# Windowed attention in a fused two-block kernel: four heads of one key head a step, values split into one stationary tile, score matmuls ordered by issue edges

## The chip, the core and the metric

The kernel runs on one core of one Trainium2 chip. The engines that matter here are TensorE (PE: matmuls and transposes, with its own sequencer for weight loads, PEld), VectorE (DVE), ScalarE (ACT) and SyncE (SP, which issues the DMAs). The metric is the device time of one launch in microseconds; three runs of the kernel before took 3067.52, 3069.00 and 3069.83 us, median 3069.0.

## The reference

512 tokens of 1024 channels pass two hybrid layers and then a second block (gated MLP mixing, a gated linear recurrence, a feed-forward part), all in float32. In each hybrid layer a convolution branch, a retention branch and a windowed attention branch read the same normalised input, are gated, added and projected. The change touches the attention branch alone:

```python
def window_attention_branch(q, k, v, gate, q_norm_g, k_norm_g, sink, positions):
    G = ATTN_HEADS // ATTN_KV_HEADS          # 16 // 4
    T = ATTN_BLOCK                           # 128
    q = rotary(rms_norm(q.reshape(B, S, ATTN_HEADS, HEAD_DIM), q_norm_g), ...)
    k = rotary(rms_norm(k.reshape(B, S, ATTN_KV_HEADS, HEAD_DIM), k_norm_g), ...)
...
    s = jnp.einsum('bhgnqj,...', qb, kwin) * (HEAD_DIM ** -0.5)   # 128 queries x 3 blocks of keys
    s = jnp.where(valid, s, -1e30)           # |kpos - qpos| <= 128
    m = jnp.maximum(jnp.max(s, axis=-1, keepdims=True), sink_l)
    p = jnp.exp(s - m)
    p = p / (jnp.sum(p, axis=-1, keepdims=True) + jnp.exp(sink_l - m))
    o = jnp.einsum('bhgnqj,bnjhd->bnqhgd', p, vwin)
    return o.reshape(B, S, ATTN_HEADS * HEAD_DIM) * jax.nn.silu(gate)
```

Sixteen query heads of 64 share four key and value heads, four to one. A block of 128 queries sees its own block of keys and the two beside it: 256 keys for the first and the last block, 384 for the two between.

## The kernel before

**Arithmetic.** Every float32 operand of a matmul is held as two parts, hi and lo, whose product sum `mm3` (L172 to L174) forms with three matmuls: hi by hi, hi by lo, lo by hi. A "dense" matmul below is one of these, a 128x128 stationary tile by 512 columns. `split` makes the two parts from PSUM: a cast on ACT (L205) and a subtraction on DVE (L206). Weights arrive by DMA in chunks of 128x1024 and are split in the same way by ACT (L149) and DVE (L150).

**Attention.** A layer calls `att_core(l, g)` twice (g = 0, 1), here "first core" (A) and "second core" (B). A core has eight steps, one for each of four query blocks n and two groups pp of four heads, and is a pipeline of three stages. In iteration `it` of its loop stand, in the order of the code: the value matmuls V of step it-2 with the gate product (four `stt` of 64x128, L213), the transposes T (L771) and splits of step it-1, and the score matmuls S (L792) of step it with its softmax. S of a step is 12 matmuls of 256 or 384 columns that contract 64 rows, into four PSUM tiles, one a head, two query tiles of two heads each; heads of both key heads of a call stand in one step, since the key tile holds one key head on its upper 64 partitions and the other on its lower 64. Softmax: a fused mask-add and row maximum on DVE (L794), the maximum against the sink (nm, L213, and es, L210, 128x4), four exps on ACT with row sums (L223), the exp of the sink, sum and reciprocal (L210, L808), and the scaling of four probability tiles, two on DVE (L217), two on ACT (L223). T turns a block of 128 keys of four heads, four 128x128 transposes into one PSUM tile, and a split of 128x512 follows. V multiplies for each block of keys the transposed probabilities (512 columns, four heads) by the values of two key heads, three matmuls by `mm3`; the upper half of the product is valid for two heads and the lower half for the other two, which is why the gate product goes in halves. After the loop four `ya` tiles are split and later read by the branch's output projection ("ao").

**What sets the order.** Every `yield` hands control to a weaver, which places 24 dense matmuls of the convolution branch between two iterations. A scheduler then orders each engine's instructions by readiness and priority from the order of the code, so that the final order on an engine need not be that of the code; each engine then works its list strictly in order. From the second core on the 31 taps of the depthwise convolution (`stt` of 128x4xx to 512 from SBUF, L213) are fed to DVE in small portions. PSUM has three pools: mm (2 buffers, names pm), acc (4, pa: scores among others) and misc (2, pi: transposes and values). `tc.issue_after(x)` puts the instructions made inside it behind x.

`att_kv` and `att_kT` make keys and values: four PSUM tiles of tokens give values in `av` (two pairs of hi and lo tiles) and, through norm and rotation, keys that `att_T` (L673) transposes into two key tiles a layer.

The lines that the change replaces in the loop are these:

```python
vh, vl = av[jb // 2]
self.mm3(ps, vh[:, c:c + 128], vl[:, c:c + 128], ph, pl, x == 0, x == len(pt) - 1)
for i in range(4):
    hs, p = hss[i // 2], 2 * pp + i % 2
    self.stt(ya[p][hs, ns], sg[p][hs, ns], 0.5, ps[hs, i * 128:i * 128 + 128], ALU.mult, ALU.mult)
```

## Time and profile before

| | |
|---|---|
| runs | 3067.52, 3069.00, 3069.83 us, median 3069.0 |
| the profiled execution | 3067.16 us, its span 3065.4 us |
| PE busy | 3022.8 us, 99% of the span, 13996 matmuls |
| DVE busy | 2078.2 us, 68% |
| ACT busy | 1130.5 us, 37% |
| four stretches with attention cores | 85.6, 87.3, 85.6 and 87.3 us |

The span goes from the first to the last recorded instruction; the execution's own time is 1.8 us longer. Busy time counts an engine from an instruction's start to its end, and matmul ends are modelled: a matmul that starts 0.23 us after its predecessor is shown with 0.39. So the share of PE says that it always had something under way, and how fast it went is read from the distances between starts. In a row of the timeline stand the start in us from the span's beginning, the duration, engine, line, operation, tiles, shape and count; a last bracket gives the idle time before it and what ended that.

### The profile page before, as it was taken

Reading aid. Unit: us, or ns where it says so; the run is one execution under the profiler, and the core shown is the slowest. Engines: PE = TensorE matmul, PEld = TensorE weight load, DVE = VectorE, ACT = ScalarE, POOL = GpSimd, SP = SyncE. Lnnn points to the kernel's source line nnn. Section 1 sums busy time; section 2 is a strip of 40 time slices with the busy share of each in tenths; the row PEclk is TensorE's granted clock in tenths of the full one; section 3 lists DMA queues with packets and bytes.
Section 4 is the critical chain, followed back from the end, with each engine's and each line's share of the span. In section 5 each row is a group of like instructions: output and inputs, shape, how many; then the busy total and the mean of one; then the engine's idle time right before and its main releaser. Section 6 shows DMA issues by size and latency. Waiting matters only on the chain.

```text
span 3065.4 us, 36069 instructions
## 1 busy us (share of the span) xinstructions
PE 3022.8 (99%) x13996; PEld 2470.4 (81%) x13996; DVE 2078.2 (68%) x3787; ACT 1130.5 (37%) x1783; POOL 0.2 (0%) x4
## 2 busy tenths in 40 slices
PE   8999999999999999999999999999999999999998
PEld 6777888887888877788888788887888888788887
DVE  7778897877444776889787764467776754753326
ACT  4545223334233444532333433333543332422222
POOL 0000000000000000000000000000000000000000
PEclk9999999999999999999999999999999999999999
DMA  4121322221233321122222132254222223422234
GB/s 163 63 69 49 97 89 76 83 76 63 95 98 129 117 76 62 62 83 97 71 74 76 63 103 96 97 173 143 90 90 69 65 74 123 161 96 99 98 110 151
DMA packets 83980, 288.99 MB, mean 94 GB/s; under 512 B 9440, under 2 KB 9696, under 8 KB 83680
## 3 DMA queue, kind: packets, MB, share of 16 engines
q1 hardware_dynamic: 83808, 286.68, 28.3%
q8 instruction: 110, 1.80, 0.2%
q14 instruction: 62, 0.51, 0.1%
HBM read 282.45 MB, written 4.19 MB: 94 GB/s over the span
## 4 chain that ended last, share of the span: by engine, by line
PE 90%; DVE 7%; ACT 2%; issue 1%; DMA 1%; SPq 0%; DVEq 0%; ACTq 0%
PE pm L172 20%; PE pm L174 20%; PE pm L173 20%; PE pa L172 6%; PE pa L174 6%; PE pa L173 6%; DVE lo L150 1%; DVE s L213 1%; PE pi L771 1%; PE pa L792 1%; PE pi L172 1%; DVE s L210 1%; PE pi L174 1%; PE pi L173 1%; ACT s L223 1%
## 5 line engine op out<-in xcount | busy, mean ns | idle before, releaser
L172 PE MATMUL pm<-s,hi 128*128 128x512 f32 x2848 | 1115.1, 392 | 1.9 <-ACT hi L149 1.2
L173 PE MATMUL pm<-s,hi 128*128 128x512 f32 x2848 | 1113.9, 391 | 0.0
L174 PE MATMUL pm<-s,lo 128*128 128x512 f32 x2848 | 1110.7, 390 | 0.5 <-DVE lo L150 0.5
L149 ACT CAST hi<-raw 128x1024 fp32r<-128x1024 f32 x497 | 523.2, 1053 | 1394.4 <-PE pm L173 761.2
L150 DVE TENSOR_TENSOR lo<-raw,hi 128x1024 fp32r<-128x1024 f32 x500 | 610.1, 1220 | 491.0 <-ACT hi L149 485.4
L172 PEld LDWEIGHTS pm<-s,hi 128*128 128x128 f32 x2848 | 534.5, 188 | 117.1 <-issue 3.5
L174 PEld LDWEIGHTS pm<-s,lo 128*128 128x128 f32 x2848 | 534.7, 188 | 113.1 <-issue 2.2
L173 PEld LDWEIGHTS pm<-s,hi 128*128 128x128 f32 x2848 | 534.8, 188 | 110.1 <-issue 1.7
L213 DVE SCALAR_TENSOR_TENSOR s<-s,m,s 128x497 f32<-128x497 f32 (+10 forms) x528 | 390.2, 742 | 11.4
L172 PE MATMUL pa<-hi,s 128*128 128x512 f32 x830 | 329.2, 397 | 9.3 <-ACT hi L147 6.7
L173 PE MATMUL pa<-lo,s 128*128 128x512 f32 x830 | 326.9, 394 | 4.8 <-DVE lo L150 4.8
L174 PE MATMUL pa<-hi,s 128*128 128x512 f32 x830 | 325.6, 393 | 0.0
L213 DVE SCALAR_TENSOR_TENSOR s<-s,pm 128x512 f32<-128x512 f32 x164 | 112.0, 683 | 147.4 <-PE pm L174 147.0
L172 PEld LDWEIGHTS pa<-hi,s 128*128 128x128 f32 x830 | 156.8, 189 | 43.0 <-ACT hi L147 6.7
L173 PEld LDWEIGHTS pa<-lo,s 128*128 128x128 f32 x830 | 157.1, 189 | 38.3 <-DVE lo L150 7.5
L174 PEld LDWEIGHTS pa<-hi,s 128*128 128x128 f32 x830 | 156.8, 189 | 31.8
L205 ACT CAST s<-s 128x512 fp32r<-128x512 f32 x184 | 110.4, 621 | 178.8 <-DVE s L213 139.1
L206 DVE TENSOR_TENSOR s<-s,s 128x512 fp32r<-128x512 f32 x184 | 123.0, 687 | 29.0 <-ACT s L205 28.2
L210 DVE TENSOR_TENSOR s<-s,s 128x512 f32<-128x512 f32 (+2 forms) x178 | 114.1, 662 | 1.7
L223 ACT ACTIVATE s<-s 128x512 f32<-128x512 f32 (+1 forms) x130 | 79.4, 628 | 89.9 <-DVE s L210 25.2
L223 ACT ACTIVATE s<-pa,m 128x256 f32<-128x256 f32 (+2 forms) x136 | 69.3, 524 | 77.4 <-DVE m L213 74.7
L213 DVE SCALAR_TENSOR_TENSOR s<-s,s 128x512 f32<-128x512 f32 (+1 forms) x130 | 88.1, 685 | 7.8 <-ACT s L223 6.3
(155 smaller groups left out, 2376.2 us busy)
## 6 DMA issues: line engine op xcount, KB each, us to landing
raw<-w SPq DMA_DIRECT2D x509, 512.0 KB, 3.3
s<-xT SPq DMA_DIRECT2D x16, 256.0 KB, 5.4
xd<-s SPq DMA_DIRECT2D x8, 256.0 KB, 2.0
s<-xd SPq DMA_DIRECT2D x8, 256.0 KB, 5.7
out<-s SPq DMA_DIRECT2D x8, 256.0 KB, 2.8
s<-c_ln_g SPq DMA_DIRECT2D x6, 256.0 KB, 4.4
s<-c_ln_b SPq DMA_DIRECT2D x6, 256.0 KB, 4.9
ckt<-ck SPq DMA_DIRECT2D x1, 1344.0 KB, 6.3
```

What stands on the lines that cost most here:

```text
L149: self.A.copy(h, raw)
L150: self.V.tensor_tensor(out=l, in0=raw, in1=h.bitcast(F32), op=ALU.subtract)
L172: T.matmul(out, lhsT=lh, rhs=rh, start=start, stop=False)
L173: T.matmul(out, lhsT=lh, rhs=rl, start=False, stop=False)
L174: T.matmul(out, lhsT=ll, rhs=rh, start=False, stop=stop)
L205: self.A.copy(h, src)
L206: self.V.tensor_tensor(out=l, in0=src, in1=h.bitcast(F32), op=ALU.subtract)
L210: return self.V.tensor_tensor(out=out, in0=a, in1=b, op=op)
L213: return self.V.scalar_tensor_tensor(out=out, in0=a, scalar=s, in1=b, op0=op0, op1=op1)
L223: return self.A.activation(out, a, f, bias=bias, scale=scale, **kw)
L771: T.transpose(ps[:, i * 128:i * 128 + 128], pr[i][:, x * 128:x * 128 + 128], self.ck("ident"))
L792: T.matmul(ps[:, 0:w], lhsT=a[hs, ns], rhs=b[hs, j0:j1], start=first, stop=last)
```

## The change

The steps of a core become (n, kv): the four query heads of one key head. Both halves of a score pair, 64 rows above and 64 below, then need the same key head on both halves of the partitions, so `twice` writes each key head two times side by side (8 ACT copies a layer) and `att_T` transposes four key tiles a layer instead of two.

Values are stored as one tile a token block, hi and lo of one key head side by side in 128 columns. One stationary tile then gives the product with hi in the upper 64 partitions and with lo in the lower 64; two matmuls, with the hi and the lo part of the probabilities, replace the three (the product lo by lo is formed too). The two halves are on different partitions and have to be added: for each 256 of the 512 columns ACT copies one half across to a slot `y` and DVE adds the other (64x256). The gate product is two `stt` of 128x128. The columns of the weights of queries, gate and the rows of the output projection stay in their natural order.

In the code of an iteration T and its splits now stand behind the scores and the softmax. `issue_after` chains every score matmul behind the one before, the first behind the last dense or value matmul that the code made (`self.dense`), and the transposes, and the first `mm3` of a following `fm`, behind the last score matmul (`self.pe`).

```diff
+    def behind(self, on=True):
+
+
+        return self.tc.issue_after(self.pe.ins) if on and self.pe is not None else nullcontext()
+
     def mm3(self, out, lh, ll, rh, rl, start, stop):
         T = self.T
         T.matmul(out, lhsT=lh, rhs=rh, start=start, stop=False)
         T.matmul(out, lhsT=lh, rhs=rl, start=False, stop=False)
-        T.matmul(out, lhsT=ll, rhs=rh, start=False, stop=stop)
+        self.dense = T.matmul(out, lhsT=ll, rhs=rh, start=False, stop=stop)
 
     def fm(self, key, cols, rhs, blocks=None, ts=None, pool=None):
...
-            self.mm3(ps, wh, wl, rh, rl, k == 0, k == len(rhs) - 1)
+            with self.behind(k == 0):
+                self.mm3(ps, wh, wl, rh, rl, k == 0, k == len(rhs) - 1)
...
+    def twice(self, xs):
+
+        out = []
+        for x in xs:
+            y = self.slot()
+            yr, xr = y.rearrange("p (h x d) -> p h x d", x=2, d=64), x[:, 0:256].rearrange("p (h d) -> p h d", d=64)
+            for i in range(2):
+                self.A.copy(yr[:, :, i, :], xr)
+            out.append(y)
+        return out
...
+        for t in range(NT):
+            v, r = self.slot(F32R), self.r[:, t:t + 1]
+            vr = v.rearrange("p (h x d) -> p h x d", x=2, d=64)
+            pv = ps[t][:, 256:512].rearrange("p (h d) -> p h d", d=64)
+            self.act(vr[:, :, 0, :], pv, AF.Copy, scale=r)
+            self.stt(vr[:, :, 1, :], pv, r, vr[:, :, 0, :].bitcast(F32), ALU.mult, ALU.subtract)
+            self.av.append(v)
...
+        ks, self.kT = self.twice(ks), []
+        for p in range(4):
...
-        iters = [(n, pp) for n in range(NT) for pp in range(2)]
+        iters = [(n, kv) for n in range(NT) for kv in range(2)]
...
-                    c = (jb % 2) * 256 + g * 128
-                    vh, vl = av[jb // 2]
-                    self.mm3(ps, vh[:, c:c + 128], vl[:, c:c + 128], ph, pl, x == 0, x == len(pt) - 1)
-                ns = slice(n * 128, n * 128 + 128)
-                for i in range(4):
-                    hs, p = hss[i // 2], 2 * pp + i % 2
-                    self.stt(ya[p][hs, ns], sg[p][hs, ns], 0.5, ps[hs, i * 128:i * 128 + 128], ALU.mult, ALU.mult)
...
-            if 0 <= it - 1 < len(iters):
...
-                s2[it - 1] = pt
...
+                    v = av[jb][:, c:c + 128]
+                    T.matmul(ps, lhsT=v, rhs=ph, start=x == 0, stop=False)
+                    self.dense = T.matmul(ps, lhsT=v, rhs=pl, start=False, stop=x == len(pt) - 1)
+
+                y = self.slot()
+                for u in range(2):
+                    cs, o = slice(u * 256, u * 256 + 256), hss[1 - u]
+                    self.A.copy(y[hss[u], 0:256], ps[o, cs])
+                    self.tt(y[hss[u], 0:256], y[hss[u], 0:256], ps[hss[u], cs], ALU.add)
+                for x in range(2):
+                    p = 2 * kv + x
+                    self.stt(ya[p][:, ns], sg[p][:, ns], 0.5, y[:, x * 128:x * 128 + 128], ALU.mult, ALU.mult)
...
+                kh, kl = self.kT[2 * g + kv]
                 sps = [None] * 4
+                self.pe = self.dense
                 for x in range(2):
-                    qh, ql = qT[2 * pp + x]
-                    kh, kl = kT
+                    qh, ql = qT[2 * kv + x]
                     both = [self.acc(), self.acc()]
                     sps[x], sps[2 + x] = both
                     for a, b, first, last in ((qh, kh, True, False), (qh, kl, False, False), (ql, kh, False, True)):
                         for ps, hs in zip(both, hss):
-                            T.matmul(ps[:, 0:w], lhsT=a[hs, ns], rhs=b[hs, j0:j1], start=first, stop=last)
+                            with self.behind():
+                                self.pe = T.matmul(ps[:, 0:w], lhsT=a[hs, ns], rhs=b[hs, j0:j1], start=first, stop=last)
...
+            if 0 <= it - 1 < len(iters):
+                n, kv = iters[it - 1]
+                pr = s1.pop(it - 1)
+                j0 = max(0, n - 1)
+                pt = []
+                for x in range(min(NT, n + 2) - j0):
+                    ps = self.misc()
+                    for i in range(4):
+                        with self.behind():
+                            T.transpose(ps[:, i * 128:i * 128 + 128], pr[i][:, x * 128:x * 128 + 128], self.ck("ident"))
+                    h, lo = self.split(ps)
+                    pt.append((j0 + x, h, lo))
+                s2[it - 1] = pt
+            yield
+        self.pe = None
...
-        mats["aq", l] = x["w_in"][l][:, O_AQ + idx]
-        mats["ag", l] = x["w_in"][l][:, O_AG + idx]
-        mats["ao", l] = x["w_attn_out"][l][idx]
+        mats["aq", l] = x["w_in"][l][:, O_AQ:O_AQ + D]
+        mats["ag", l] = x["w_in"][l][:, O_AG:O_AG + D]
+        mats["ao", l] = x["w_attn_out"][l]
```

Three places of the final order follow; a name is the kind of tile, its number and its buffer (pi, pa and pm are PSUM tiles of the misc, acc and mm pools, s a slot, hi, lo and raw a weight chunk, m a small tile). First PE around the fourth turn of the first core, before: the last dense matmuls, the values V of a step with three blocks of keys, then the scores.

```order
L174 MATMUL pm259_1360<-s82_419,lo17_1135 128x512
L172 MATMUL pi261_1393<-s239_1297,s58_363 128x512
L173 MATMUL pi261_1393<-s240_1298,s58_363 128x512
L174 MATMUL pi261_1393<-s239_1297,s59_364 128x512
L172 MATMUL pi261_1393<-s242_1306,s58_363 128x512
L173 MATMUL pi261_1393<-s243_1307,s58_363 128x512
L174 MATMUL pi261_1393<-s242_1306,s59_364 128x512
L172 MATMUL pi261_1393<-s245_1315,s60_369 128x512
L173 MATMUL pi261_1393<-s246_1316,s60_369 128x512
L174 MATMUL pi261_1393<-s245_1315,s61_370 128x512
L792 MATMUL pa273_1436<-s117_665,s147_847 128x384
L792 MATMUL pa274_1437<-s117_665,s147_847 128x384
```

The same place now: the last four transposes T, then V, then S.

```order
L180 MATMUL pm272_1392<-s82_419,lo17_1166 128x512
L839 MATMUL pi269_1383<-ckt_115,s234_1235 128x128
L839 MATMUL pi269_1383<-ckt_115,s235_1236 128x128
L839 MATMUL pi269_1383<-ckt_115,s236_1237 128x128
L839 MATMUL pi269_1383<-ckt_115,s237_1238 128x128
L775 MATMUL pi274_1425<-s264_1370,s58_363 128x512
L776 MATMUL pi274_1425<-s265_1371,s58_363 128x512
L775 MATMUL pi274_1425<-s267_1379,s59_366 128x512
L776 MATMUL pi274_1425<-s268_1380,s59_366 128x512
L775 MATMUL pi274_1425<-s270_1388,s60_369 128x512
L776 MATMUL pi274_1425<-s271_1389,s60_369 128x512
L805 MATMUL pa278_1441<-s124_686,s157_877 128x384
L805 MATMUL pa279_1442<-s124_686,s157_877 128x384
```

V is six matmuls where it was nine, and the transposes that fill pi269, with the split that makes s270 and s271 of it, stand directly in front of the V that reads s270 and s271. In before the tiles that V reads were transposed ahead of the 24 dense matmuls.

Next DVE in a step of the first core, before: the splits s267 and s270, masks and maxima (ISA), nm, es, the sum, the reciprocal, the two scalings.

```order
L206 TENSOR_TENSOR s267_1422<-pi265_1416,s266_1421 128x512
L206 TENSOR_TENSOR s270_1431<-pi268_1425,s269_1430 128x512
L794 ISA pa275_1446,m271_1434<-pa275_1446,ckt_115 128x384
L794 ISA m271_1434 128x1
L794 ISA pa276_1447,m271_1434<-pa276_1447,ckt_115 128x384
L794 ISA m271_1434 128x1
L213 SCALAR_TENSOR_TENSOR m277_1456<-m271_1434,m89_465 128x4
L210 TENSOR_TENSOR m278_1458<-vkt_91,m277_1456 128x4
L210 TENSOR_TENSOR m272_1435<-m272_1435,m278_1458 128x4
L808 RECIPROCAL m272_1435<-m272_1435 128x4
L217 TENSOR_SCALAR s279_1460<-s279_1460,m272_1435 128x384
L217 TENSOR_SCALAR s281_1462<-s281_1462,m272_1435 128x384
```

DVE in such a step now, from nm on.

```order
L220 SCALAR_TENSOR_TENSOR m232_1231<-m226_1209,m89_465 128x4
L217 TENSOR_TENSOR m233_1233<-vkt_91,m232_1231 128x4
L217 TENSOR_TENSOR m227_1210<-m227_1210,m233_1233 128x4
L823 RECIPROCAL m227_1210<-m227_1210 128x4
L224 TENSOR_SCALAR s234_1235<-s234_1235,m227_1210 128x384
L224 TENSOR_SCALAR s236_1237<-s236_1237,m227_1210 128x384
L213 TENSOR_TENSOR s240_1256<-pi238_1250,s239_1255 128x512
L213 TENSOR_TENSOR s243_1265<-pi241_1259,s242_1264 128x512
L151 TENSOR_TENSOR lo19_1394<-raw19_1065,hi19_1393 128x1024
L213 TENSOR_TENSOR s246_1274<-pi244_1268,s245_1273 128x512
L217 TENSOR_TENSOR s250_1317<-s250_1317,pi249_1310 64x256
```

The two or three splits of the preceding step's transposes stood among the masks; now they stand behind the scalings of the step, and a weight's lo between them. The last row is the first of the new adds.

Last, PE at the end of the second core, before: the last V, the last product of the gate (pm583), and the first matmuls of the output projection (pm585; pm611 in the rows of now).

```order
L173 MATMUL pi574_2999<-s573_2996,s60_369 128x512
L174 MATMUL pi574_2999<-s572_2995,s61_370 128x512
L172 MATMUL pm583_3026<-s82_419,hi36_2747 128x512
L173 MATMUL pm583_3026<-s83_420,hi36_2747 128x512
L174 MATMUL pm583_3026<-s82_419,lo36_2748 128x512
L172 MATMUL pm585_3064<-s336_1736,hi37_2863 128x512
L173 MATMUL pm585_3064<-s337_1737,hi37_2863 128x512
L174 MATMUL pm585_3064<-s336_1736,lo37_2864 128x512
L172 MATMUL pm585_3064<-s338_1740,hi37_2863 128x512
```

And now:

```order
L776 MATMUL pi599_3036<-s595_3024,s60_369 128x512
L178 MATMUL pm611_3102<-s360_1782,hi37_2899 128x512
L179 MATMUL pm611_3102<-s361_1783,hi37_2899 128x512
L775 MATMUL pi599_3036<-s597_3032,s61_372 128x512
L180 MATMUL pm611_3102<-s360_1782,lo37_2900 128x512
L776 MATMUL pi599_3036<-s598_3033,s61_372 128x512
L178 MATMUL pm611_3102<-s601_3048,hi37_2899 128x512
L179 MATMUL pm611_3102<-s602_3049,hi37_2899 128x512
L180 MATMUL pm611_3102<-s601_3048,lo37_2900 128x512
L178 MATMUL pm611_3102<-s603_3052,hi37_2899 128x512
```

Three gate matmuls and the projection's products of the first core's outputs (s336 to s341 are such) stood between the last V and the projection's use of the second core's outputs. Now the gate is ahead, the last product of the first core's outputs (s360, s361) stands between the last V matmuls, and the first products of the second core's outputs (s601 to s604) follow the last V directly.

## Rows read from the trace of the kernel before

**Rows 1.** The page, busy time of the engines with share of the span and instructions.

```profile
PE 3022.8 (99%) x13996; PEld 2470.4 (81%) x13996; DVE 2078.2 (68%) x3787; ACT 1130.5 (37%) x1783; POOL 0.2 (0%) x4
```

**Rows 2.** The page, the chain of work that ended last, shares by engine.

```profile
PE 90%; DVE 7%; ACT 2%; issue 1%; DMA 1%; SPq 0%; DVEq 0%; ACTq 0%
```

**Rows 3.** The view by stretches, the four stretches in which attention cores run: from and to, length, busy time and instructions of PE, PEld, DVE, ACT and POOL, granted clock of PE, DMA share, GB/s.

```profile
90.10:175.70 85.60, 83.67 (x439) 64.83 (x439) 60.37 (x181) 50.13 (x125) 0.00 (x0) 1.00 0.15 50
219.30:306.60 87.30, 86.72 (x445) 66.37 (x445) 72.26 (x200) 50.72 (x126) 0.00 (x0) 1.00 0.15 51
1106.20:1191.80 85.60, 83.68 (x438) 64.80 (x438) 60.34 (x181) 50.17 (x125) 0.00 (x0) 1.00 0.15 50
1235.50:1322.80 87.30, 86.70 (x444) 66.29 (x444) 72.19 (x200) 50.70 (x126) 0.00 (x0) 1.00 0.16 50
```

**Rows 4.** The timeline of PE in the first two of these stretches: starts of score pieces (L792; a piece ends where the asked window or another kind of matmul ends it, so the counts differ), one group of transposes (L771) and the dense matmul behind it, the last value matmul of each core (L174, pi) and a dense one three later.

```profile
90.09 0.97 PE L792 MATMUL pa<-s,s 64*128 64x256 f32 x12
...
106.12 0.79 PE L792 MATMUL pa<-s,s 64*128 64x384 f32 x5
...
115.41 0.61 PE L792 MATMUL pa<-s,s 64*128 64x384 f32 x4
...
130.13 0.66 PE L771 MATMUL pi<-ckt,s 128*128 128x128 f32 x4
130.54 0.47 PE L173 MATMUL pm<-s,hi 128*128 128x512 f32 x1
...
150.04 0.50 PE L792 MATMUL pa<-s,s 64*128 64x256 f32 x4
...
160.88 0.73 PE L792 MATMUL pa<-s,s 64*128 64x256 f32 x7
...
171.37 0.39 PE L174 MATMUL pi<-s,s 128*128 128x512 f32 x1
...
235.52 0.61 PE L792 MATMUL pa<-s,s 64*128 64x384 f32 x3
...
245.88 0.79 PE L792 MATMUL pa<-s,s 64*128 64x384 f32 x6
...
280.70 0.73 PE L792 MATMUL pa<-s,s 64*128 64x256 f32 x7
...
291.55 0.73 PE L792 MATMUL pa<-s,s 64*128 64x256 f32 x7
...
302.25 0.39 PE L174 MATMUL pi<-s,s 128*128 128x512 f32 x1
...
302.93 0.39 PE L174 MATMUL pm<-s,lo 128*128 128x512 f32 x1
```

**Rows 5.** The timeline of DVE in one 384-wide step of the first core: the step's last two masks, nm, the sum behind the exps, the scalings, a weight's lo, four gate products.

```profile
142.87 0.56 DVE L794 CUSTOM_DVE_ANT_0 pa<-pa,ckt 128x384 f32<-128x384 f32 x1
...
143.34 0.60 DVE L794 CUSTOM_DVE_ANT_0 pa<-pa,ckt 128x384 f32<-128x384 f32 x1
...
144.03 0.16 DVE L213 SCALAR_TENSOR_TENSOR m<-m,m 128x4 f32<-128x4 f32 x1
...
146.71 0.16 DVE L210 TENSOR_TENSOR m<-m,m 128x4 f32<-128x4 f32 x1 [2.33 <-ACT m L223]
...
147.12 0.75 DVE L217 TENSOR_SCALAR s<-s,m 128x384 f32<-128x384 f32 x2
148.53 1.23 DVE L150 TENSOR_TENSOR lo<-raw,hi 128x1024 fp32r<-128x1024 f32 x1 [0.65 <-ACT hi L149]
149.71 0.99 DVE L213 SCALAR_TENSOR_TENSOR s<-s,pi 64x128 f32<-64x128 f32 x4
```

**Rows 6.** The timeline of ACT in the same step: a weight's cast and the two scalings.

```profile
147.44 1.05 ACT L149 CAST hi<-raw 128x1024 fp32r<-128x1024 f32 x1 [0.76 <-PE pm L173]
148.40 1.11 ACT L223 ACTIVATE s<-s,m 128x384 f32<-128x384 f32 x2
```

**Rows 7.** Groups of instructions over the whole span, shapes apart: count, busy us, mean ns of one, idle time before them.

```profile
L206 DVE TENSOR_TENSOR s<-pi,s 128x512 fp32r<-128x512 f32 x100 | 66.4, 686 | 11.8 <-ACT s L205 11.0
L205 ACT CAST s<-pi 128x512 fp32r<-128x512 f32 x100 | 56.9, 588 | 51.9 <-PE pi L771 44.6 <-PE pi L673 6.7
L213 DVE SCALAR_TENSOR_TENSOR s<-s,pi 64x128 f32<-64x128 f32 x128 | 31.5, 282 | 4.6 <-PE pi L174 4.0
...
L223 ACT ACTIVATE m<-m 128x4 f32<-128x4 f32 x32 | 6.8, 213 | 0.0
...
L210 DVE TENSOR_TENSOR s<-pa,vkt 128x256 f32<-128x256 f32 x8 | 3.3, 414 | 0.0
L223 ACT ACTIVATE s<-pa 128x256 f32<-128x256 f32 x8 | 2.6, 382 | 0.0
```

**Rows 8.** The timeline of DVE behind the second step's masks in the second core: nm, convolution taps (128x510), the sum behind the exps.

```profile
222.59 0.15 DVE L213 SCALAR_TENSOR_TENSOR m<-m,m 128x4 f32<-128x4 f32 x1
...
223.44 1.54 DVE L213 SCALAR_TENSOR_TENSOR s<-s,m,s 128x510 f32<-128x510 f32 x2
224.89 0.16 DVE L210 TENSOR_TENSOR m<-m,m 128x4 f32<-128x4 f32 x1
```

**Rows 9.** A place in the second block where PE stood still: the timeline of PE, and the view by stretches (columns as in rows 3).

```profile
2075.04 1.86 PE L363 MATMUL pi<-ckt,s 128*128 128x128 f32 x8 [1.97 <-DVE s L213]
...
2075.00:2079.00 4.00, 3.96 (x15) 3.45 (x16) 3.11 (x8) 1.16 (x5) 0.00 (x0) 0.57 0.00 0
```

More of the change, by code (lines that the diff above doesn't have):

```diff
@@ L1 @@
 import math
-from contextlib import ExitStack
+from contextlib import ExitStack, nullcontext
 import numpy as np
@@ L698, in att_kT @@
         yield from nrm
-        self.kT = []
-        for p in range(2):
+        ks, self.kT = self.twice(ks), []
+        for p in range(4):
             self.kT.append(self.att_T(ks, p))
@@ L742, in att_core @@
         T = self.T
[L743 to L745 removed]
+        qT, av, sg = self.qT, self.av, self.asg
         ya = [self.slot() for _ in range(4)]
[L747 removed]
+        iters = [(n, kv) for n in range(NT) for kv in range(2)]
         hss = [slice(0, 64), slice(64, 128)]
```

39 lines of the change are left out of this document (10 added, 29 removed).

## The prediction

> **What bounds the kernel now.** First the page's busy shares: PE is busy 99% of the span, DVE 68%, ACT 37% [rows 1], and the chain that ended last lies to 90% on PE [rows 2]. That speaks for any change that takes matmuls away. But it is an average, so I next cut out the four stretches in which attention cores run, two a layer [rows 3]: 85.6 and 87.3 us, the same in both layers, 345.8 us in all. There ACT works 50 us and DVE 60 and 72 us. PE looks full, yet part of that is pace: a dense 128x512 matmul follows the last in 0.227 us (302.25 to 302.93 are three) [rows 4]. The first stretch has 439 matmuls, 263 after 96 scores and 80 transposes: 263 x 0.227 = 59.7. A group of four transposes takes 0.41 to the start of the matmul behind it (130.13 to 130.54), an unbroken 256-wide score piece 0.97 [rows 4]; a 384-wide one I estimate at 1.3, since its first four take 0.61 against 0.50 (115.41, 150.04). That makes 59.7 + 20 x 0.41 + 4 x 0.97 + 4 x 1.3 = 77.0, so 8.6 us of this stretch are switching and waits, some 35 in the four.
>
> The third view is one step on DVE and ACT: the last masks at 142.87 and 143.34, nm at 144.03, then DVE sits 2.33 us until four exps are through, and sum, reciprocal and scaling follow at 146.71 to 147.12 [rows 5, 6]. The softmax round trip is longer than any single instruction, and who waits behind it decides this change.
>
> **The change part by part.** Steps are numbered 0 to 7 in a core; S, T, V are a step's score, transposed and value matmuls.
>
> *Value matmuls.* A step multiplies its values once per block of keys; the 80 such blocks lose one of three matmuls each: 80 x 0.227 = 18.2 us of PE. *Score pieces.* No transpose splits them: up to 35 us in the four cores. *Keys twice.* 16 more transposes, 4 x 0.41 = 1.6 us on PE; the eight ACT copies and two splits a layer lie under att_q's 96 matmuls and cost nothing there, 2 us if they don't. *Reordered weight columns* are host data, and SP keeps its 585 rows; nothing.
>
> *Output.* Four 64x128 instructions become two ACT copies, two DVE adds (64x256) and two 128x128 products. Nearest rows: ACT 128x256 0.382, DVE 128x256 0.414; bounds 0.213 and 0.588 for the copy, 0.282 and 0.686 for the add [rows 7]. I take the two nearest.
>
> *The order.* In before the splits of step k-1's transposes stand ahead of the masks of step k. In after T(k-1) and its splits come behind S(k): on ACT behind exps(k), on DVE behind scaling(k). V(k-1) needs them, and S(k+1) is behind V(k-1) on PE. So one turn of the loop holds a whole softmax and all splits, with only 24 dense matmuls (5.45) to cover it. From the end of a last V, w = 384:
>
> - copy 0.04 to 0.42, add 0.46, mask 0.80, second copy 0.91 to 1.29 (it waits for the first add), add 1.41, mask 1.82, two products to 2.70, masks 2.70 and 3.17, nm 0.69 later (143.34 to 144.03) at 3.86;
> - exps, sum: 2.68 (144.03 to 146.71) to 6.54; scaling 0.41 later, 6.95 [rows 5];
> - ACT: two scalings from 7.0, 1.03 (pitch 0.515, from 1.11 for two), cast of T2 8.0 to 8.6, weight cast 8.5 to 9.55 (1.05) [rows 6];
> - DVE: lo of the weight 9.6, 1.18 to the next (148.53 to 149.71) [rows 5], last split 10.77 to 11.46 (0.69) [rows 7]; last V 11.50, end 11.9.
>
> PE's own work in such a step is 1.3 + 3 x 0.41 + 24 x 0.227 + 6 x 0.227 = 9.3, so it waits 2.6 us. Before, steps 3 to 5 took (150.04 - 115.41)/3 = 11.54 and (280.70 - 245.88)/3 = 11.61 [rows 4]. The removed matmuls buy nothing here.
>
> [...]
>
> The other steps by the same chain (A: first core of a layer, B: second):
>
> - S(0) to S(2): A 0.97 + 5.45, then behind S(1) four masks to 8.8, lo to 10.0, nm to sum 2.30 (222.59 to 224.89) [rows 8], 0.5 to the scalings, two of them estimated at 0.9 from 1.11 for the 384 wide [rows 6], cast 0.59, split 0.69 [rows 7], last V and the start of S 0.3: 15.3 against 106.12 - 90.09 = 16.03. In B conv taps (two in 1.54, pitch 0.66) [rows 8] stand in that chain, two behind nm more than the wait hides and one before each reciprocal: 17.0 against 235.52 - 219.30 = 16.22 (the stretch begins with S(0)).
> - S(2) to S(3): no third split, but lo 0.6 late: A 10.2 against 9.29; in B two taps ahead, lo before nm and a tap before the reciprocal: 12.75 against 10.36.
> - S(3) to S(6): A 12.5 + 2 x 11.9 = 36.3 against 34.63; B 36.4 against 34.82.
> - S(6) to S(7), 256 wide: nm 3.45, sum 5.75, scalings to 7.1, two casts to 8.4, split 9.2, last V and S: 9.7 against 10.84 and 10.85.
> - S(7) to the last V: T, V wait for each other with little dense work left: 13.45 in A against 171.37 - 160.88 = 10.49, but 11 more dense matmuls lie ahead of it (2.5 us), so 0.5 more. In B 13.5 against 10.70; then four ao products wait for the last outputs: copy, add, two products, cast and split in turn end the 24th at 5.7, where 28 matmuls took 6.36 without a wait. 2.2 more.
>
> A: -0.7 + 0.9 + 1.7 - 1.1 + 0.5 = +1.3. B: 0.8 + 2.4 + 1.6 - 1.1 + 2.2 = +5.9. Two layers 14.4, keys 1.6: +16 us. The profiled execution took 3067.2, so 3083; the median of the runs is 1.8 above it, so 3084 or 3085. I say 3084.
>
> **The rivals.**
>
> *PE stays the bound (faster).* If the hand-offs overlap better than my chain, what PE no longer does shows: at most 18.2 + 35 less 1.6 and some 3 for S-to-T switches, 49 us, 3020. It decides where a turn falls under 9.3 us in the long steps. For it: PE is 90% of the chain. Against it: ACT and DVE run in issue order, and the softmax trip of 2.68 with what stands behind it cannot shrink to that. More likely is part of it: copies and adds at their low ends (0.6 a turn, 24 turns, -14), the short steps half a microsecond nearer to PE's own 8 to 9 (-6) and no wait for ao (-4): 3060.
>
> *A wash.* The long turns cost no more than before (-6.6) and the ends of A and B lose nothing (-5.4): of +16 some 4 stay, 3073. For it: every term is a few tenths of a step. Against it: they lean one way.
>
> [...]
>
> *The change doesn't do what it says:* the order has every 12 scores in one piece and 160 value matmuls where 240 were, so this has no chance of its own.
>
> **How the numbers follow.** My forecast (3075 and above without a clock fall) 0.5; clock 0.05; wash 0.25; PE bound, in part or whole, 0.2. The unknown copies and adds move the sum by -14 (all low) to about +20 (all high, two copies 0.21 and two adds 0.27 longer, less what a mask hides), so my forecast's own range is 3070 to 3104; the wash and the part gain take it down to 3058, and the full gain is left out. A measurement tells 0.2%, 6 us, from no change: faster 0.2, same 0.25, slower 0.55.
>
> **What would show it.** Right: PE idle of 2 to 3 us a long step in front of V's last two matmuls and T3, released by DVE splits and ACT casts; long steps at 11.9; DVE's wait for exps still 2.3; a wait of 2 to 3 us in ao's first product of each layer. Value matmuls 160 where 240 were, unbroken scores near 1.3. Wrong: long steps under 11, or PE's idle in the four stretches near the 5 us of before; or a granted clock below 1.00 there.

## The result and the profile after

The changed kernel takes 3090.56 us (median of 4 runs, 3088.25 to 3097.31) against 3068.26 of the kernel before (4 runs): ratio 1.0074, 95% interval 1.0061 to 1.0086, 22 us slower. 3084 was forecast. Its profiled execution took 3089.08 us, span 3087.1, 21.7 longer than before. The page first: busy times and the chain that ended last.

```profile
PE 3010.0 (98%) x13932; PEld 2449.9 (79%) x13932; DVE 2094.8 (68%) x3791; ACT 1155.1 (37%) x1867; POOL 0.2 (0%) x4
...
PE 85%; DVE 10%; ACT 4%; issue 1%; DMA 1%; SPq 0%; DVEq 0%; ACTq 0%
```

PE works 12.8 us less than in [rows 1], yet its share of the chain falls from 90% [rows 2] to 85%: it waits for DVE and ACT. The waits of PE say where (us in all, times, the longest):

```profile
PE pi L775 <- DVE s L213: 10.1, 18, 1.6
PE pi L776 <- DVE s L213: 9.7, 16, 0.8
PE pi L839 <- DVE s L217: 6.8, 17, 1.2
...
PE pi L839 <- DVE s L213: 6.5, 15, 0.9
...
PE pm L178 <- ACT s L212: 2.0, 2, 1.0
```

L775 and L776 are the value matmuls V, waiting for the splits (L213); L839 are the transposes T, waiting for a PSUM buffer that an add of the output (L217) or a split (L213) frees. The last row is the output projection, behind the split of the last outputs.

The four stretches, each from the first score to the last V (columns as in [rows 3]; those ran 4.3 us on behind the last V, and the dense work within a stretch differs too, so the lengths don't compare directly):

```profile
91.79:178.59 86.80, 77.09 (x412) 57.98 (x412) 59.33 (x172) 51.44 (x135) 0.00 (x0) 1.00 0.15 49
223.70:314.27 90.57, 81.37 (x421) 60.85 (x420) 71.93 (x192) 51.51 (x135) 0.00 (x0) 0.98 0.17 55
1119.32:1206.12 86.80, 77.13 (x412) 58.00 (x412) 59.33 (x172) 51.43 (x135) 0.00 (x0) 1.00 0.15 49
1251.24:1341.93 90.69, 81.42 (x421) 60.87 (x420) 71.92 (x192) 51.50 (x135) 0.00 (x0) 0.98 0.16 53
```

In each PE is idle for 9.2 to 9.7 us, where [rows 3] show 0.6 to 1.9. In the two second cores the granted clock is 0.98; the part on the rivals returns to that. One turn of the loop, from scores to scores, on PE (start, duration, engine, line, operation, tiles, count, idle before and its releaser):

```profile
142.41 1.32 PE L805 MATMUL pa<-s,s 64*128 64x384 f32 x12
143.65 0.66 PE L839 MATMUL pi<-ckt,s 128*128 128x128 f32 x4
144.46 0.63 PE L839 MATMUL pi<-ckt,s 128*128 128x128 f32 x4 [0.15 <-DVE s L217]
...
151.00 0.66 PE L839 MATMUL pi<-ckt,s 128*128 128x128 f32 x4 [0.45 <-DVE s L213]
152.02 0.50 PE L775 MATMUL pi<-s,s 128*128 128x512 f32 x1 [0.37 <-DVE s L213]
...
154.10 0.50 PE L776 MATMUL pi<-s,s 128*128 128x512 f32 x1 [0.66 <-DVE s L213]
154.54 0.86 PE L805 MATMUL pa<-s,s 64*128 64x256 f32 x10
```

on DVE:

```profile
142.91 0.41 DVE L217 TENSOR_TENSOR s<-s,pi 64x256 f32<-64x256 f32 x1 [0.40 <-ACT s L781]
143.25 0.55 DVE L807 CUSTOM_DVE_ANT_0 pa<-pa,ckt 128x384 f32<-128x384 f32 x1
...
143.89 0.42 DVE L217 TENSOR_TENSOR s<-s,pi 64x256 f32<-64x256 f32 x1
144.34 0.57 DVE L807 CUSTOM_DVE_ANT_0 pa<-pa,ckt 128x384 f32<-128x384 f32 x1
...
146.50 0.16 DVE L220 SCALAR_TENSOR_TENSOR m<-m,m 128x4 f32<-128x4 f32 x1
...
149.19 0.16 DVE L217 TENSOR_TENSOR m<-m,m 128x4 f32<-128x4 f32 x1 [2.32 <-ACT m L230]
...
150.26 0.68 DVE L213 TENSOR_TENSOR s<-pi,s 128x512 fp32r<-128x512 f32 x1
...
152.22 1.23 DVE L151 TENSOR_TENSOR lo<-raw,hi 128x1024 fp32r<-128x1024 f32 x1 [0.26 <-ACT hi L150]
153.37 0.68 DVE L213 TENSOR_TENSOR s<-pi,s 128x512 fp32r<-128x512 f32 x1
```

and on ACT:

```profile
142.51 0.37 ACT L781 COPY s<-pi 64x256 f32<-64x256 f32 x1 [1.97 <-PE pi L776]
143.36 0.36 ACT L781 COPY s<-pi 64x256 f32<-64x256 f32 x1 [0.48 <-DVE s L217]
146.70 0.58 ACT L230 ACTIVATE s<-pa,m 128x384 f32<-128x384 f32 x1 [2.98 <-DVE m L220]
...
149.03 0.60 ACT L212 CAST s<-pi 128x512 fp32r<-128x512 f32 x1
```

The turn is 154.54 - 142.41 = 12.13 us. In it PE waits 1.63 us (the brackets above). T's first block is transposed by 144.3, but its cast starts at 149.03, behind the exps, though ACT stood idle 2.98 us in between; the last split ends at 154.05 and the last V starts at 154.10.

### The profile page after: what moved, and what is told of

It reads as the page before. It is cut to its first block, busy times and chain, and to the rows that moved or that the text cites. A ratio compares the mean times of both kernels' runs of the same rounds, so it can differ in the third digit from the quotient of the medians.

```text
span 3087.1 us, 36015 instructions
## 1 busy us (share of the span) xinstructions
PE 3010.0 (98%) x13932; PEld 2449.9 (79%) x13932; DVE 2094.8 (68%) x3791; ACT 1155.1 (37%) x1867; POOL 0.2 (0%) x4
## 4 chain that ended last, share of the span: by engine, by line
PE 85%; DVE 10%; ACT 4%; issue 1%; DMA 1%; SPq 0%; DVEq 0%; ACTq 0%
PE pm L178 19%; PE pm L179 19%; PE pm L180 19%; PE pa L178 7%; PE pa L180 7%; PE pa L179 7%; DVE s L220 2%; ACT s L230 2%; DVE lo L151 2%; DVE pa L807 1%; DVE s L217 1%; PE pa L1099 1%; ACT hi L150 1%; ACT s L212 1%; DVE s L213 1%
## 5 line engine op out<-in xcount | busy, mean ns | idle before, releaser
L213 DVE TENSOR_TENSOR s<-s,s 128x512 fp32r<-128x512 f32 x184 | 123.2, 687 | 30.3 <-ACT s L212 29.2
L217 DVE TENSOR_TENSOR s<-s,s 128x512 f32<-128x512 f32 (+2 forms) x178 | 114.1, 662 | 1.7
L220 DVE SCALAR_TENSOR_TENSOR s<-s,s 128x512 f32<-128x512 f32 (+2 forms) x194 | 103.8, 554 | 8.2 <-ACT s L230 6.7
```

The source lines that it names most:

```text
L213: self.V.tensor_tensor(out=l, in0=src, in1=h.bitcast(F32), op=ALU.subtract)
L217: return self.V.tensor_tensor(out=out, in0=a, in1=b, op=op)
L220: return self.V.scalar_tensor_tensor(out=out, in0=a, scalar=s, in1=b, op0=op0, op1=op1)
```

## The experiments

Each was run in 3 rounds (the last in 4) beside the kernel before. "Long step" is the mean of steps 3 to 5 of the first core, (start of step 6's scores - start of step 3's) / 3 on PE's timeline; before it is (150.04 - 115.41) / 3 = 11.54 [rows 4]. "PE idle" is PE's idle time in all four cores, each from its first score to the end of its last V; before it is 5.0.

| kernel | median us | ratio to before, 95% interval | step 3, step 6 | long step | PE idle |
|---|---|---|---|---|---|
| changed | 3090.56 | 1.0074 (1.0061 to 1.0086) | 117.49, 154.54 | 12.35 | 37.9 |
| e1 old place of T and splits | 3067.53 | 0.9994 (0.9985 to 1.0004) | 118.83, 151.43 | 10.87 | 12.7 |
| e2 order alone | 3074.48 | 1.0020 (1.0010 to 1.0030) | 118.69, 154.28 | 11.86 | 23.1 |
| e3 no edges | 3066.48 | 0.9990 (0.9981 to 0.9999) | 115.65, 147.16 | 10.50 | 8.7 |
| e4 no halves | 3052.15 | 0.9947 (0.9932 to 0.9962) | 117.21, 149.96 | 10.92 | 17.5 |
| e5 casts in the gap | 3052.20 | 0.9949 (0.9933 to 0.9966) | 116.14, 148.49 | 10.78 | 18.1 |
| e6 output late | 3077.36 | 1.0029 (1.0018 to 1.0040) | 119.65, 153.95 | 11.43 | 26.9 |
| e7 old place, output late | 3097.32 | 1.0093 (1.0078 to 1.0108) | 116.84, 151.19 | 11.45 | 32.0 |
| e8 third matmul | 3102.29 | 1.0111 (1.0096 to 1.0126) | 118.28, 155.82 | 12.51 | 30.9 |
| e9 gap, short output | 3047.62 | 0.9930 (0.9915 to 0.9945) | 116.49, 148.08 | 10.53 | 15.4 |
| e10 short output | 3081.94 | 1.0043 (1.0026 to 1.0059) | 117.11, 153.02 | 11.97 | 27.6 |
| e11 old place, no halves | 3054.24 | 0.9952 (0.9937 to 0.9967) | 117.46, 151.15 | 11.23 | 5.4 |
| e12 copies together | 3050.47 | 0.9935 (0.9922 to 0.9949) | 118.12, 149.82 | 10.57 | 16.8 |

**The parts apart: e1 to e4 and e11.**

e1 puts T and the splits back ahead of the scores (the block is moved whole; T loses its edge):

```diff
+            if 0 <= it - 1 < len(iters):
+                n, kv = iters[it - 1]
...
+                s2[it - 1] = pt
             if it < len(iters):
                 n, kv = iters[it]
```

> The changed kernel with the transposes and splits of the preceding step put back ahead of the scores and the softmax, as before the change; the value tile, the keys written twice, the output path and the score chain stay. If the place of the splits is the cause (they stand behind the exps and the scalings, V waits for them, the next scores wait for V), PE loses its waits of some 2.7 us a long turn: a long step (scores to scores) falls from 12.13 to 9.5 to 11, PE's waits for DVE in the four attention stretches from 34 us to under 12, and the kernel comes out at 3035 to 3062, faster than before. If the output path (copies across partitions and adds) is the cause, long steps stay near 12 and the time stays at 3080 to 3095.

Measured: 3067.53, as before the change and outside both cases; the long step, 10.87, and PE's waits for DVE in the four cores, 9.5 us where the changed kernel has 33.1, fit the first. The 22 us are gone with the place, but the value matmuls' 18.2 us don't appear either. Part of them went into PE's idle time (12.7 us against 5.0 before) and part into the keys (1.5 us a layer, as shown below); where the rest went was not followed. Without its edges this kernel has the same order of instructions on every engine, so e1 is also the change without its order: the value tile, the keys written twice and the output path together gain nothing that the runs can tell.

e2 is the kernel before with the change's place and edges alone:

```diff
-            if 0 <= it - 1 < len(iters):
...
+                            with self.behind():
+                                self.pe = T.matmul(ps[:, 0:w], lhsT=a[hs, ns], rhs=b[hs, j0:j1], start=first, stop=last)
...
                 s1[it] = pr
+            if 0 <= it - 1 < len(iters):
```

> The kernel before with nothing but the change's order: transposes and splits behind scores and softmax, and the issue edges on the scores; values by three matmuls and the output by four 64x128 products as before. If the order is the cause, PE waits in front of the values as in the changed kernel: long steps near 11.7 (the output path costs 0.4 less than copies and adds), the time 3080 to 3092. If the output path is the cause, long steps are at or under the 11.5 of before, the time 3055 to 3070.

Measured: 3074.48, between the two cases; the long step, 11.86, is near the first. The second row is the wait that was forecast, V (L176) for the splits (L211). The first and larger is T (L819), which waits for the PSUM buffer that a split frees:

```profile
PE pi L819 <- DVE s L211: 10.0, 16, 1.0
PE pi L176 <- DVE s L211: 7.0, 12, 1.2
```

The order alone costs 0.1 to 0.3%, and the other parts alone nothing; together they cost 0.74%. So most of the loss appears only when both are there.

e3 takes the edges away and leaves the place:

```diff
-        return self.tc.issue_after(self.pe.ins) if on and self.pe is not None else nullcontext()
+        return self.tc.issue_after(self.pe.ins) if False else nullcontext()
```

> The changed kernel without its issue-order edges; everything else, the place of transposes and splits too, as in the change. The scheduler then puts scores of the next step ahead of the last value matmuls again. If the loop over the values is the cause (scores in order behind values that wait for splits), a long step falls to 10.5 to 11.5 and the time to 3055 to 3078. If the broken score pieces that the edges prevent are dearer than that wait, the time rises above 3095. If only the splits' place counts, whatever the scores do, the time stays within 5 us of 3090.

Measured: 3066.48, long step 10.50, both within the first case; PE's idle time falls from 37.9 to 8.7 us. The scheduler puts some or all of a step's twelve scores ahead of the V that waits, in pieces again; cutting the loop at that place is worth 3090.6 - 3066.5 = 24 us, broken scores and all.

e4 leaves out copies and adds, so the halves aren't summed:

```diff
-                y = self.slot()
-                for u in range(2):
...
-                    self.stt(ya[p][:, ns], sg[p][:, ns], 0.5, y[:, x * 128:x * 128 + 128], ALU.mult, ALU.mult)
+                    self.stt(ya[p][:, ns], sg[p][:, ns], 0.5, ps[:, x * 128:x * 128 + 128], ALU.mult, ALU.mult)
```

> The changed kernel without the copies and adds of the output: the two gate products read the 128x128 value product straight from PSUM, so the sum of upper and lower halves is left out. It prices the output path alone. By the chain of my sum it holds the masks up by about 1.3 us a turn (the first mask can start 0.7 after the values' end instead of 0.85, the third at 1.4 instead of 2.9): long steps 10.7 to 11.0, the time 3055 to 3065. If the splits' place is the whole cause and the masks are hidden, long steps stay at 12 and the time at 3085 to 3092. If the output path is the whole cause, the time falls to the 3050 that the removed value matmuls give, or under.

Measured: 3052.15, just under the range of the first case; the long step, 10.92, is in it. e11 leaves out the same work in e1.

> The run with the old place of transposes and splits, and without the copies and adds of the output (the sum of upper and lower halves is left out). It tells why that run stood at 3067 though its value matmuls are 18.2 us less than before. If the output path ate the gain, the time falls to 3035 to 3050 and long steps to 9.6 to 10.3. If the broken score pieces and the two PSUM buffers hold it anyway, the time stays over 3060.

Measured: 3054.24, between the two cases. The long step does not fall (11.23 against 10.87); the gain stands at the cores' ends, from step 7's scores to the last V 9.98 and 10.10 us where e1 has 13.47 and 14.49, a part of it dense work that moved. Over the whole kernel two copies and two adds a step cost 3090.6 - 3052.2 = 38.4 us in the change's order and 3067.5 - 3054.2 = 13.3 in the old one, and without them the order costs nothing (3052.2 against 3054.2). Up to 3.4 of the 13.3 are TensorE's clock, by an estimate of 2 x 4 x 0.43: e1 has two stretches of 4 us at a granted clock of 0.57 at the end of its first cores (168 to 172, 1185 to 1189), and the mean granted clock of its profiled execution is 0.997 where e11 has 0.998. The copies and adds are the same instructions in both orders. What differs, by the rows of the turn above, is that in the change's order they stand between the last V and the masks, on the loop that the next V waits for. Their durations over the whole span:

```profile
L217 DVE TENSOR_TENSOR s<-s,pi 64x256 f32<-64x256 f32 x64 | 26.7, 417 | 14.6 <-ACT s L781 13.6
L781 ACT COPY s<-pi 64x256 f32<-64x256 f32 x64 | 23.4, 366 | 49.3 <-PE pi L776 32.3 <-DVE s L217 16.7
```

They are the 0.414 and 0.382 that the prediction took from [rows 7], within 0.02; in all they are 50 us of work.

**What the removed matmuls were worth: e8.**

```diff
                     T.matmul(ps, lhsT=v, rhs=ph, start=x == 0, stop=False)
+                    T.matmul(ps, lhsT=v, rhs=pl, start=False, stop=False)
```

> The changed kernel with a third value matmul put back for every block of keys (the low part of the probabilities is multiplied a second time, so the result counts it twice): the matmuls that the change takes away, 18.2 us of PE. If they were hidden in the loop, as I said, only the one behind the last split shows, 0.23 in each of 32 steps less what waits anyway: plus 4 to 8 us, 3094 to 3099. If PE's work does bound a part of the steps, plus 15 to 18, 3105 to 3109.

Measured: 3102.29, 11.7 more, between my two cases. The turn of the profile above goes from 12.13 to 12.37, that is by one matmul of three, as said. The rest is lost in steps with two blocks of keys and at the cores' ends: step 6 to 7 goes from 10.17 to 10.84.

**Moving the work within the loop: e5, e6, e7, e10.**

e5 issues two casts ahead of the exps and two subtractions behind nm:

```diff
+                if pt is not None:
+                    casts()
                 nm = self.small([128, 4], tag="nm")
...
+                if pt is not None:
+                    subs()
                 pr = [self.slot() for _ in range(4)]
```

> The changed kernel with one thing moved: of the preceding step's first two transposed blocks the ACT casts are issued ahead of the exps (into the 3 us in which ACT waits for the maxima) and the DVE subtractions between nm and the sum (into the 2.3 us in which DVE waits for the exps); only a third block's split stays behind the scalings. If V waits because those splits stand behind the softmax, two of three are gone from the loop: long steps fall from 12.13 to 9.6 to 10.6 and the time to 3030 to 3060. If the loop is held by the masks behind copies and adds alone, long steps stay over 11.5 and the time over 3075.

Measured: 3052.20, as expected, with the long step, 10.78, just over its range. Nothing is left out and scores stay in one piece: 38 us under the change (some 3 of them from the clock, by an estimate of 0.001 x 3087 from the mean granted clocks of the two profiled executions, 0.998 in e5 and 0.997 in the changed kernel), 16 under the kernel before. V hardly waits any more (2.4 us in two waits at L775, 0.7 in three at L776); T does, for the output's adds and the subtractions, which free PSUM buffers (L798 is T, L217 the adds and subtractions):

```profile
PE pi L798 <- DVE s L217: 14.4, 24, 1.0
...
PE pi L775 <- DVE s L217: 2.4, 2, 1.2
```

e6 leaves the splits and puts the output behind nm; e7 does that in e1:

```diff
+                if it >= 2:
+                    out()
                 pr = [self.slot() for _ in range(4)]
```

> The changed kernel with copies, adds and gate products of the output issued behind nm, where DVE waits for the exps, in place of ahead of the masks; nothing is left out. If their price in the changed kernel (38 us by the run that leaves out the copies and adds) is their place ahead of the masks, most of it comes back: nm some 1.3 us earlier after the last value matmul, long steps 10.5 to 11.0, the time 3050 to 3065. If it is their work on DVE and ACT wherever they stand, or the value tile in PSUM held longer delays the second block's transposes, long steps stay over 11.5 and the time over 3078.

> Both moves: transposes and splits ahead of the scores as before the change, and copies, adds and gate products behind nm. If the two places are the whole cause, neither splits nor output stand in the loop from values to values, PE's own 9.3 us a long step bound it: steps 9.4 to 10.2, the time 3025 to 3050, under every kernel so far. If DVE's and ACT's work itself is the limit, it stays at the 3067 of the run with the old place.

Measured: 3077.36 and 3097.32, both misses. In e6 a turn starts with the scores at 142.10. On DVE a weight's lo now stands ahead of the first mask, and the first add ahead of nm:

```profile
142.12 1.22 DVE L151 TENSOR_TENSOR lo<-raw,hi 128x1024 fp32r<-128x1024 f32 x1
...
145.28 0.41 DVE L217 TENSOR_TENSOR s<-s,pi 64x256 f32<-64x256 f32 x1
145.61 0.15 DVE L220 SCALAR_TENSOR_TENSOR m<-m,m 128x4 f32<-128x4 f32 x1
```

So nm comes 3.5 us behind the start of the scores, where it was 4.1, and not 1.3 earlier. On ACT the second copy waits for that first add, and the exps stand behind the copy:

```profile
145.72 0.36 ACT L784 COPY s<-pi 64x256 f32<-64x256 f32 x1 [3.15 <-DVE s L217]
146.11 0.58 ACT L230 ACTIVATE s<-pa,m 128x384 f32<-128x384 f32 x1
```

The exps come 4.0 us behind the start of the scores, 4.3 in the changed kernel: 0.3 is left of the 0.6. In e7 the values' tile holds one of the two misc buffers through all this, and the other has to serve three blocks of transposes in turn (the second and third start at 271.94 and 274.01, 0.1 behind the subtraction of the block ahead); ACT's casts wait for each:

```profile
272.58 0.59 ACT L212 CAST s<-pi 128x512 fp32r<-128x512 f32 x1 [1.38 <-PE pi L799]
274.64 0.59 ACT L212 CAST s<-pi 128x512 fp32r<-128x512 f32 x1 [1.48 <-PE pi L799]
```

Three blocks at a pitch of 2.06 are 6 us. My expectation had counted DVE and ACT and forgotten the buffer. That the buffer is the cause is read from these rows; no run had a third one. Part of e7's 30 us over e1 is the clock: 168 to 175 and 1199 to 1206 stand at 0.52 and 0.51, 318 to 322 and 1349 to 1353 at 0.57, by an estimate of 7 x 0.48 + 7 x 0.49 + 8 x 0.43 up to some 10 us of lost pace where e1 has 3.4; the mean granted clock is 0.995 against 0.997.

e10 gives the copies slots of their own, lets the adds write a third and puts only the gate products behind nm:

```diff
-                y = self.slot()
+                z, y0, y1 = self.slot(), self.slot(), self.slot()
...
+                if it >= 2:
+                    gate()
                 pr = [self.slot() for _ in range(4)]
```

> The changed kernel, splits behind the softmax as in the change, with the same shorter output path (copies in slots of their own, gate products behind nm). The PSUM tile of the values is freed early and not late, so this tells the place of the output path from the buffer that it holds. By the chain nm comes 0.7 to 0.9 earlier after the last value matmul: long steps 11.2 to 11.5, the time 3066 to 3076. If the work itself is the price, long steps stay at 12.1 and the time at 3086 to 3093.

Measured: 3081.94, about half of what was expected: the turn goes from 12.13 to 11.76, by about the time of the two gate products (0.49 us on DVE).

**A faster version: e9 and e12.** e9 is e5 with e10's output path.

> The kernel with the casts in the gap, and a shorter output path: the two ACT copies go to slots of their own and both adds write a third, so that the second copy doesn't wait for the first add, and the two gate products are issued behind nm. In the kernel with the casts in the gap PE's waits were left with the second block's transposes, 0.6 us each in 24 steps (14.4 us), whose PSUM buffer the second add frees. If that add is now 0.4 to 0.7 earlier, those waits fall to under 5 us and nm comes 0.6 to 0.9 earlier: long steps 9.7 to 10.2, the time 3030 to 3043. If DVE's work in the turn is the limit and not its order, the time stays within 5 us of 3052.

Measured: 3047.62, long step 10.53: the fastest with the whole computation, 21 us under the kernel before. But the expectation's first case failed: T still waits 13.5 us for the adds, and the time lies within 5 us of 3052, which was the second case. The second copy again starts behind the first add (a slot of its own didn't help), and the first add itself starts late, behind a weight's lo:

```profile
137.97 0.37 ACT L781 COPY s<-pi 64x256 f32<-64x256 f32 x1
137.98 1.23 DVE L151 TENSOR_TENSOR lo<-raw,hi 128x1024 fp32r<-128x1024 f32 x1 [0.21 <-ACT hi L150]
139.13 0.41 DVE L217 TENSOR_TENSOR s<-s,pi 64x256 f32<-64x256 f32 x1
139.56 0.36 ACT L781 COPY s<-pi 64x256 f32<-64x256 f32 x1 [1.22 <-DVE s L217]
```

So most of the 1.22 us is the weight's lo; in the changed kernel, where nothing stood ahead of the add, the second copy waited 0.48. Second copy and first add both read partitions 0 to 63 of one PSUM tile. In these rows the two reads don't overlap, the add ends at 139.54 and the copy starts at 139.56; what an overlap would do was not tried.

e12 issues both copies ahead of both adds:

```diff
                     self.A.copy(y[hss[u], 0:256], ps[o, cs])
+                for u, y in enumerate((y0, y1)):
+                    cs = slice(u * 256, u * 256 + 256)
                     self.tt(z[hss[u], 0:256], y[hss[u], 0:256], ps[hss[u], cs], ALU.add)
```

> The last kernel (casts in the gap, short output path) with both ACT copies issued ahead of both DVE adds. Slots of their own did not free the second copy: it still starts only when the first add has ended (1.22 us later than it could), and both read the same 64 partitions of the same PSUM tile, so the programmer's framework puts one engine's read behind the other's. If that shared PSUM tile is what makes copy, add, copy, add a chain, then issued in this order the second copy starts right behind the first (0.35 to 0.40 later), the two adds stand back to back, the second block's transposes wait 0.3 us less a step, and the time is 3036 to 3044. If the wait has another cause, the second copy stays 1 us or more behind the first and the time stays within 3 us of 3047.6.

Measured: 3050.47, not faster than e9 (the intervals overlap): the mechanism of the first case with the time of the second. Issued in this order, the copies and the adds stand in pairs, so the shared tile had made the chain:

```profile
139.79 0.75 ACT L781 COPY s<-pi 64x256 f32<-64x256 f32 x2
...
139.80 1.23 DVE L151 TENSOR_TENSOR lo<-raw,hi 128x1024 fp32r<-128x1024 f32 x1 [0.21 <-ACT hi L150]
140.94 0.84 DVE L217 TENSOR_TENSOR s<-s,pi 64x256 f32<-64x256 f32 x2
```

But in this step the adds start at 140.94 behind a weight's lo of 1.2 us, not behind the copies (done at 140.54), and PE's waits for them stay (14.2 us in 24 waits, 13.5 in e9). So in this step it is the weight's lo, and no longer the chain, that holds the adds; moving the weight's split was not tried.

## Why the prediction was right

**The loop was the right step.** Its chain for a 384-wide turn, counted from the start of the scores behind the last V (142.41), against the trace: nm 3.86, measured 4.09; sum 6.54, measured 6.78; cast of T2 8.0, measured 8.27; weight's lo 9.6, measured 9.81; last split 10.77, measured 10.96; the next scores 11.9, measured 12.13 (all us). The 0.23 builds up from the first copy to the third mask and runs through. That this chain is the bound is shown by the runs that break it at one place each: e3 at the scores, e1 and e5 at the splits, e4 at the output. DVE's wait for the exps is 2.32, forecast 2.3; the scores in one piece take 143.65 - 142.41 = 1.24, forecast 1.3.

**The sum by place**, in one layer, in us more than before, each from a place on PE to the same place in before:

| stretch | first core, forecast | measured | second core, forecast | measured |
|---|---|---|---|---|
| S(0) to S(2) | -0.7 | -0.8 | +0.8 | +0.1 |
| S(2) to S(3) | +0.9 | +1.2 | +2.4 | +2.5 |
| S(3) to S(6), the long turns | +1.7 | +2.4 | +1.6 | +2.4 |
| S(6) to S(7) | -1.1 | -0.7 | -1.1 | -0.7 |
| S(7) to the second core's S(0), or to the projection's 25th matmul | +0.5 | +0.6 | +2.2 | +2.8 |
| sum | +1.3 | +2.7 | +5.9 | +7.1 |

The sums are (223.70 - 91.79) - (219.30 - 90.09) and (320.11 - 223.70) - (308.59 - 219.30). Ahead of the first scores the change costs 91.79 - 90.09 = 1.7, forecast 0.8 for the keys. Together that is 11.5 a layer against 8.0. Two layers make 23; the place of [rows 9] in the second block comes 2097.90 - 2075.04 = 22.9 later. Behind that place the granted clock was 0.57 for 4 us before, by an estimate of 4 x 0.43 a loss of 1.7, and 1.00 in the changed kernel, which takes 1.2 us less from there to the end: 21.7 at the end, forecast 16. So the forecast was low by a quarter. The largest part of what it missed is in the long turns, which it had 0.2 to 0.3 too short each; the rest is in the steps beside them and in the keys; one term, S(0) to S(2) of the second core, was too high by 0.7 and hid a part of that, which was luck.

The keys can be read apart, since e2 has the change's order and each key once. From the program's 201st matmul to the first scores before takes 90.09 - 59.18 = 30.91 us, e2 93.06 - 62.16 = 30.90 and the changed kernel 91.79 - 59.38 = 32.41: the keys cost 1.5 a layer, nearly double the forecast. The transposes that came in twos among dense matmuls are not what was underrated: a pair takes 0.14 to the next dense matmul and that one 0.31 in place of 0.23 (70.26, 70.40, 70.71), so two pairs are about what the prediction took for four. What the rest is stays open.

**The signs.** Of what the prediction named as signs of being right, the long turn (12.13 to 12.14 in the last two of three, 11.9 forecast), DVE's wait and the whole score pieces came. PE's idle time in a long turn is 1.63 us and not 2 to 3, and stands in front of two blocks of T and of the first and the last V matmul, all of it released by DVE. Of the signs of being wrong one came: the granted clock was 0.98 in two stretches. The last outputs were where the prediction put them. The first product waits 0.98 us and not 2 to 3, but three behind it wait too (0.22, 0.20 and 0.23), and the projection's 24 matmuls are done by 320.11, 5.7 behind the end of the last V (314.38), as forecast:

```profile
313.87 0.51 PE L776 MATMUL pi<-s,s 128*128 128x512 f32 x1
315.35 0.50 PE L178 MATMUL pm<-s,hi 128*128 128x512 f32 x1 [0.98 <-ACT s L212]
```

**The removed matmuls "buy nothing here"** was too strong. By e8 they bought 0.24 of 0.68 us in a long turn, and over all steps 11.7 of 18.2 us, which the new waits ate.

**What it didn't say** is how much of the loss hangs on the output path. It had the copies and adds in its chain, ahead of the masks, but named the order as the cause. The order alone costs 0.2% (e2), and with the copies and adds left out it costs nothing (e4 against e11). Each alone is nearly harmless; in one loop they cost 22 us.

**The adds on the two halves.** The prediction's chain has 0.34 us from the start of the first add to the mask behind it and 0.41 from the second. The 0.41 was the author's estimate, and no run shows it. The changed kernel's trace has, behind the add on partitions 0 to 63, the next instruction 143.25 - 142.91 = 0.34 later, before the add has ended, and behind the add on partitions 64 to 127 144.34 - 143.89 = 0.45 later, after its end. e12's two adds, one on each half, take 0.84 where one takes 0.417. So the mask behind the second add started 0.11 us later than the one behind the first; no run prices that over the whole kernel.

**The rivals.** PE as the bound fails in the change, and e9 moves toward it, 10.53 a long step against PE's own 9.3. The wash fails. The clock, to which the prediction gave a chance of 0.05, did fall, though not in each long turn. In each second core V waited 1.55, 0.38 and 0.79 us in a row (250.09, 251.20 and 252.48 in the first layer; 1.54, 0.38 and 0.79 in the second), and then the granted clock was 0.57 for 4 us: 0.53 and 0.61 from 253, 0.64 and 0.51 from 1280, 2 us each. It fell once more, to 0.57, behind the second layer's last V (1345 to 1349). In exchange the fall of [rows 9] is not there in the changed kernel, at the same place of the program, with a wait of 1.95 us (2097.90):

```profile
253.00:255.00 2.00, 2.00 (x13) 1.56 (x13) 1.85 (x6) 0.73 (x2) 0.00 (x0) 0.53 0.66 252
255.00:257.00 2.00, 2.00 (x12) 1.96 (x11) 1.95 (x8) 0.00 (x0) 0.00 (x0) 0.61 0.00 0
...
317.00:321.00 4.00, 3.44 (x13) 2.28 (x13) 2.52 (x6) 2.65 (x4) 0.00 (x0) 1.00 0.00 0
...
1345.00:1349.00 4.00, 3.98 (x9) 2.52 (x10) 1.55 (x4) 2.12 (x4) 0.00 (x0) 0.57 0.00 0
...
2096.00:2100.00 4.00, 2.09 (x12) 1.55 (x13) 4.00 (x9) 1.15 (x4) 0.00 (x0) 1.00 0.29 114
```

By an estimate of 2.0 x 0.47 + 2.0 x 0.39 such a fall takes 1.7 us of PE's full speed, as much as the 4 x 0.43 of [rows 9]. Not all of it shows: the turn from 252.91 takes 12.97 us, and the same turn of the first core, at 1.00, 12.78 (117.49 to 130.27). Three falls in the place of one are at most 3.4 of the 22 us, and not the result's sign.

## What to carry to other kernels

In a software pipeline (steps of a loop that overlap) on engines that work their lists in order, follow one value around the loop and count what stands between its two visits to the bound engine. The same 50 us of copies and adds cost 38 us on that path and 13 off it. Look for the engine that idles inside the turn and issue there what the next turn needs: here the casts and subtractions in the waits of ACT and DVE, worth 38 us. But count the buffers first: in e7 a PSUM tile that is held for longer leaves one buffer for all transposes, and the kernel takes 30 us more than e1. Two engines that read one PSUM tile in turn can make a chain of their own (e9's second copy started 0.02 us behind the end of the first add, after a wait of 1.22), and undoing it helps only if nothing else holds the same instructions.

## What the runs showed of the hardware

Like waits of PE were followed by unlike clocks. In the second block waits of 1.97 and 1.95 us at one place were followed by a granted clock of 0.57 before the change and 1.00 after it; before, PE had also waited 0.83 us some 3 us earlier (2071.64). At the start of the output projection the changed kernel has the same three waits in both layers, 0.98, 0.22 and 0.20 us from 315.35 and 0.98, 0.23 and 0.22 from 1343.01; then the clock stood at 1.00 in the first layer and at 0.57 in the second. So here a pause of 0.98 to 1.97 us didn't settle the clock by itself. ACT's copy of 64x256 from PSUM to other partitions takes 0.366 us and its activation of 128x256 0.382 [rows 7]; DVE's add of 64x256 takes 0.417 and of 128x256 0.414: half the partitions save next to nothing.
